# Ordered operand addresses at four places, a GpSimd fold for LayerNorm's sums and a later mean, in a decoder-layer kernel on Trainium2

## The chip, the core and the metric

The kernel runs on one core of one Trainium2 chip. The core has a tensor engine (PE) for matmuls, a vector engine (DVE), a scalar engine (ACT), GpSimd (POOL) and a sync engine (SP) that here only issues DMAs. Each works through its own instructions in order and waits on semaphores for the others. The metric is device time in microseconds (us), lower is better. A kernel is timed in several runs, and one execution is recorded by the hardware profiler; the start and end of every instruction in this document come from such a record.

## What is computed

One layer of a decoder over 288 tokens: 256 of one prompt and 8 x 4 of running samples. The width is 2048, everything is float32.

```python
h = rmsnorm(x, norm1_g)
proj = einsum("btd,de->bte", h, w_in) + b_in          # 2048 -> 3072
a, gate, z = proj[..., :1024], proj[..., 1024:2048], proj[..., 2048:]
u = a * sigmoid(gate)
u_ext = concat([hist_conv, u], axis=1)
c = silu(layernorm(depthwise_causal_conv(u_ext, conv_w, conv_b), ln_g, ln_b))   # 31 taps
z_ext = concat([hist_pool, z], axis=1)
d = multiscale_pool(z_ext, pos0)                      # windows 2, 4, 8, 16
p = einsum("btgc,gce->btge", d, pool_w) * pool_scale
x = x + einsum("btm,md->btd", concat([c, p], axis=-1), w_out)
h2 = rmsnorm(x, norm2_g)
f = square(relu(einsum("btd,df->btf", h2, w_ff1)))    # 2048 -> 8192
x = x + einsum("btf,fd->btd", f, w_ff2)               # 8192 -> 2048
```

A final RMSNorm follows. The last 30 rows of `u_ext` and the last 15 of `z_ext` are outputs too. LayerNorm runs over the 1024 convolution channels.

## The kernel before

**Layout.** Channels lie on the 128 partitions, tokens along the free dimension (`T` = 288), so each product is a 128x128 weight block against a 128x288 operand. All large products go through `gemm` (line 286), whose matmul is line 310.

**Three products for one.** float32 accuracy is made from the tensor engine's fast float32r format: a weight block is split into a high part (`whi`, a rounding copy on ACT, line 260) and a low part (`wlo`, the rest), and so are the operands. For every pair of reduction blocks and every output bank `gemm` issues six products: high by high, low weight by high operand, high weight by low operand, for two blocks each (`parts`, line 296). A call with two banks has 96 products for a reduction of 2048 (48 for 1024, 12 for a pooling group).

**Where the low part of a weight comes from.** `split_part` (line 254) knows three ways: "V", a subtraction on DVE (line 265); "G", two subtractions of 128x512 on GpSimd (line 268); "D", ACT writes the negative of the high part and a DMA that GpSimd issues adds the weight from memory (lines 262 and 263). `WAYS` (line 70) lists the ways by stage, in turn for the quarter-blocks (`wr`, 512 KB) of the stage: c3 has four of them, one gemm. Buffers: six raw blocks, five high and five low ones.

**The order of the operands.** `act2` (line 121) puts the high and low parts of two reduction blocks into one tile of four slots of 288 floats (1152 bytes): low even, high even, high odd, low odd. In the default order the products read slots 1, 2, 1, 2, 3, 0. `gemm` calls an operand class 0 if it lies in slot 1 or 3, else class 1; the default order thus alternates 0, 1, 0, 1. With `classes`, a string of digits, it reorders the first products of the call: for each digit it takes the next product of that class. Before uses this once, at chunk 0, g 2 of the first MLP product (line 603), with 24 digits.

**Stages.** The first gemm makes a and gate of convolution channels 0 and 1 (192 products, while x arrives). Then the sequence of line 45: `c2`, `c3`, `c4`, ... are 128 convolution channels each (`conv_products`, `conv_pair`), `p3` to `p0` the pooling groups (`pool_group`), `P3` to `P0` their small products (`pool_products`). The 31 taps of a convolution run on DVE, one instruction a tap (line 426), put behind all urgent work by `later()`. Channels 2j and 2j+1 share the tile `cs[j]`. `sum_c`, two halves of 288, gathers the sums of the even and the odd channel blocks as they finish, on GpSimd (line 435), up to channel block 5.

Then w_out comes in two halves. The pooling half (loop at line 543, eight g of 48 products, operands `dx`) runs first. LayerNorm's statistics stand between its products, by `BETWEEN` (line 541): `ln_mean` (line 517) at g 4 before reduction block 4, `ln_sums` at g 5 before block 6, `ln_rows` at g 6 before block 4. They are f32 matmuls with a matrix of 1/1024, which sum over partitions. `ln_sums` subtracts the mean, squares, adds up and starts the root; `ln_rows` spreads the root's 288 values over all partitions. `issue_after` keeps the products that follow on PE behind each. The normalized channels (`mixc`, lines 551 to 561) are the operands `mx` of the convolution half (loop at line 566, eight g of 48 products). The MLP runs in four chunks of 2048: eight g of 96 products from `ax` to `fx`, then eight g of 96 back. The row of the second RMSNorm (`rsqrt_rows`, line 605) stands between chunk 0, g 0 and g 1.

**Who sets the order.** The Tile framework orders the instructions of each engine by priority (program order, plus what `later` adds) over a simulated timeline, and sets the semaphores. Each engine then keeps that order on the chip.

Of the kernel before, what the change touches and what calls it, by code (L numbers as in the profile page):

```python
# [12 lines left out]
ALU = mybir.AluOpType  # L13
# [17 lines left out]
N8 = DC // P  # L31
# [35 lines left out]

WAYS = {"c2": "GVGV", "c3": "GDGD", "c4": "GDGD", "p3": "GDDG", "c5": "GDGD", "c": "GGGV", "p": "GVVG", "w": "GG", "ff": "VV"}  # L70


VEC = (("norm1_g", 16), ("b_in", 24), ("conv_b", 8), ("ln_g", 8), ("ln_b", 8), ("pool_scale", 8), ("norm2_g", 16), ("norm_f", 16))
# [10 lines left out]
def trunk_kernel(ctx: ExitStack, tc: tile.TileContext, io):  # L84
# [3 lines left out]
    nc = tc.nc  # L88
# [106 lines left out]
    ones = const.tile([P, P], F32, name="ones")  # L195
# [80 lines left out]
    def split(halves, stage="ff"):  # L276

        parts = []
        for raw, src in halves:
            turns[stage] = turns.get(stage, -1) + 1  # L280
            parts.append(spl())
            ways = WAYS.get(stage) or WAYS[stage[0]]
            split_part(raw, src, *parts[-1], ways[turns[stage] % len(ways)])
# [33 lines left out]
    def each(bk):  # L317
        return [bk[:, m, :] for m in range(2)]
# [28 lines left out]
    korder = [2 * g + m for g in GROUPS for m in range(2)]  # L347
# [43 lines left out]
    cs, pcs = [], []  # L391
    sum_c = tmpp.tile([P, 2, T], F32, name="sum_c", tag="ag2", bufs=2)
# [4 lines left out]
    def conv_products(i, **kw):  # L397
        history(i)
        banks = each(bank2())
        gemm(banks, hx, **kw)  # L400
        return banks

    def conv_pair(i, banks):
        up = u_all[:, i, 0:UO]
        us = samples(u_all[:, i, UO:UL], US)
        ta, gate = [b[:, :T] for b in banks]
        for b in (gate, ta):
            nc.vector.tensor_tensor(b, b, rb, op=ALU.mult)
        tg = tmpp.tile([P, 2, T], F32, name=nm("tg"), tag="ag", bufs=2)[:, 0, :]
        nc.scalar.activation(tg, gate, AF.Sigmoid, bias=v("b_in", 8 + i))  # L410
        if i == N8 - 1:
            load_table(AF.Sqrt, tg[:, 0:1])
        for out, a, b in ((up[:, CH:UO], ta[:, :SEQ], tg[:, :SEQ]), (us[:, :, CH:US], samples(ta[:, SEQ:T], NS), samples(tg[:, SEQ:T], NS))):
            nc.vector.scalar_tensor_tensor(out=out, in0=a, scalar=v("b_in", i), in1=b, op0=ALU.add, op1=ALU.mult)
        if i % 2 == 0:
            cs.append(actp.tile([P, 2, T], F32, name=nm("c"), tag="c", bufs=4))
        c = cs[i // 2][:, i % 2, :]
        with later():
            if i % 2 == 0:
                pcs.append(cvp.tile([P, 2, SEQ], F32, name=nm("pc"), tag="cv"))  # L420
            pc = pcs[i // 2][:, i % 2, :]
            cwv = vec[:, CWO + i * CW : CWO + (i + 1) * CW]
            nc.scalar.activation(pc, up[:, 0:SEQ], AF.Identity, bias=v("conv_b", i), scale=cwv[:, 0:1])  # L423
            for w in range(1, CW):
                dst = pc if w < CW - 1 else c[:, 0:SEQ]
                nc.vector.scalar_tensor_tensor(out=dst, in0=up[:, w : w + SEQ], scalar=cwv[:, w : w + 1], in1=pc, op0=ALU.mult, op1=ALU.add)  # L426
            prd = prdp.tile([P, NB, NS, CW + 1], F32, name=nm("prd"), tag="prd")
            nc.scalar.activation(prd[:, :, :, CW], ones[:, 0 : NB * NS].rearrange("p (b t) -> p b t", t=NS), AF.Identity, bias=v("conv_b", i), scale=0.0)
            for t in range(NS):
                nc.gpsimd.tensor_tensor(prd[:, :, t, 0:CW], us[:, :, t : t + CW], cwv[:, None, :].to_broadcast([P, NB, CW]), op=ALU.mult)  # L430
            cso = c[:, SEQ:T]
            nc.vector.tensor_reduce(samples(cso, NS), prd, axis=AX.X, op=ALU.add)
            if i % 2 and 1 < i < N8 - 1:
                for m in range(2):
                    nc.gpsimd.tensor_tensor(sum_c[:, m, :], (cs[0] if i == 3 else sum_c)[:, m, :], cs[i // 2][:, m, :], op=ALU.add)


    dd = {}
# [31 lines left out]
    mixp = {}  # L470
# [24 lines left out]
        return last  # L495

    with tc.issue_after(gemm(pair0 + pair1, hx, between={15: first_sums})):
        third = conv_products(2, between={2: first_rows})
    nc.gpsimd.memset(z_all[:, :, 0:PH], 0.0)
    conv_pair(0, pair0)  # L500
    conv_pair(1, pair1)
# [13 lines left out]
    norm = {}  # L515

    def ln_mean():
        nc.vector.tensor_tensor(sum_c, sum_c, cs[-1], op=ALU.add)  # L518
        nc.vector.tensor_tensor(sum_c[:, 0, :], sum_c[:, 0, :], sum_c[:, 1, :], op=ALU.add)  # L519
        norm["mean"] = ms("pmean")[:, 0, :T]  # L520
        return nc.tensor.matmul(norm["mean"], ones, sum_c[:, 0, :], start=True, stop=True)  # L521

    def ln_sums():
        ssc = None
# [13 lines left out]
        norm["rows"], last = spread(norm["sums"])  # L538
        return last

    BETWEEN = {4: {4: ln_mean}, 5: {6: ln_sums}, 6: {4: ln_rows}}
    behind = nullcontext()
    for g in range(8):
        bk = bank2()
        with behind:
            last = gemm(each(bk), [mixp[k] for k in korder], between=BETWEEN.get(g, {}))
        behind = tc.issue_after(last) if g > 3 else nullcontext()
        x2 = xT[:, 2 * g : 2 * g + 2, :]
        nc.vector.tensor_tensor(x2, x2, bk[:, :, :T], op=ALU.add)

    mixc = []
    for j, c in enumerate(cs):
        n = tmpp.tile([P, 2, T], F32, name=nm("n"), tag="ag", bufs=2)
        nc.vector.tensor_tensor(n, c, norm["rows"][:, None, :].to_broadcast([P, 2, T]), op=ALU.mult)
        for m in range(2):
            i = 2 * j + m
# [7 lines left out]
    x1 = []  # L564
    ss2 = row("ss2")
    for g in range(8):
        bk = bank2()
        gemm(each(bk), mixc)
        x2 = xT[:, 2 * g : 2 * g + 2, :]
        nc.vector.tensor_tensor(x2, x2, bk[:, :, :T], op=ALU.add)  # L570
        if g < 4:
            a2 = halves(act2("ax", tag="p", bufs=4))
        elif g < 6:
            if g == 4:
                ax45 = zp.tile([P, N8 * ZL], F32R, name="ax45", tag="z")
                ax45 = ax45[:, 32 : 32 + 8 * T].rearrange("p (g r t) -> p g r t", g=2, r=4)
            a2 = halves(rows(ax45[:, g - 4]))
        else:
            a2 = []
            for m in range(2):  # L580
                t2 = actp.tile([P, 2, T], F32R, name=nm("ax"), tag="c", bufs=4)
                a2.append((t2[:, 1 - m, :], t2[:, m, :]))
        for m, (ah, al) in enumerate(a2):
            k = 2 * g + m
            xk = xT[:, k, :]
            nc.scalar.activation(ah, xk, AF.Copy, scale=v("norm2_g", k))
            nc.vector.scalar_tensor_tensor(out=al, in0=xk, scalar=v("norm2_g", k), in1=f32(ah), op0=ALU.mult, op1=ALU.subtract)
            x1.append((ah, al))
            if k == 0:
                nc.scalar.activation(ss2, xk, AF.Square)  # L590
            else:
                q2 = tmp("q")
                nc.scalar.activation(q2, xk, AF.Square)
                nc.gpsimd.tensor_tensor(ss2, ss2, q2, op=ALU.add)
# [4 lines left out]
    for ch in range(DFF // FCH):  # L599
        fx = []  # L600
        for g in range(FCH // 256):
            bk = bank2()
            gemm(each(bk), x1, classes="01" + "110011001100" + "01" * 5 if ch == 0 and g == 2 else "")
            if ch == 0 and g == 0:
                nc.scalar.copy(r2, rsqrt_rows([ss2], 1.0 / D))
            t = tmpp.tile([P, 2, T], F32, name=nm("t"), tag="ag", bufs=2)
            nc.vector.scalar_tensor_tensor(out=t, in0=bk[:, :, :T], scalar=0.0, in1=both(r2), op0=ALU.max, op1=ALU.mult)  # L607
            f = tmpp.tile([P, 2, T], F32, name=nm("f"), tag="ag2", bufs=2)
            nc.scalar.activation(f, t, AF.Square)
            fh, fl = act2("fx")  # L610
            nc.scalar.copy(fh, f)
            nc.vector.tensor_tensor(fl, f, f32(fh), op=ALU.subtract)
            fx += halves((fh, fl))
        last = ch == DFF // FCH - 1
        for g in range(8):
            bk = bank2()
            banks = each(bk)
            if last and g == 7:
                banks[1] = bank2()[:, 1, :]
            gemm(banks, fx, m_outer=last and g == 7)  # L620
            for m in range(2):
                k = 2 * g + m
                xk = xT[:, k, :]
                if last:
                    nc.vector.tensor_tensor(xk, xk, banks[m][:, :T], op=ALU.add)
                    if k == 0:
                        nc.scalar.activation(ssf, xk, AF.Square)
                    else:
                        qf = tmp("q")
                        nc.scalar.activation(qf, xk, AF.Square)  # L630
                        if k < KT - 1:
                            nc.vector.tensor_tensor(ssf, ssf, qf, op=ALU.add)
                    nc.scalar.activation(xk, xk, AF.Copy, scale=v("norm_f", k))
                elif m:
                    x2 = xT[:, 2 * g : 2 * g + 2, :]
                    nc.vector.tensor_tensor(x2, x2, bk[:, :, :T], op=ALU.add)  # L636
# [65 lines left out]
```

## Time and profile before

| | us |
|---|---|
| three timed runs | 1096.64, 1096.86, 1117.09 |
| median of them | 1096.86 |
| the profiled execution, whole | 1097.78 |
| its span, first to last instruction | 1096.0 |
| DVE busy | 640.9 |
| ACT busy | 477.5 |
| GpSimd busy | 179.2 |
| mean granted clock of PE, as a share | 0.994 |

How to read the profile. A group row has line, engine, operation, output<-inputs by the program's names, shape, count, then total busy time, mean ns of one, and the idle time of the engine before them with what ended it. A chain row has start, length and what, one row for a run of equal instructions with their count. A window row has the window, its length, busy time of each engine with its count, the granted clock, the DMA engines' share and GB/s; a count takes in instructions that only reach into the window. "PEld" is the loading of weights, which overlaps with PE's products; matmuls overlap too, so the pace is time over count and not the length of one. A trailing q (POOLq) is an engine's sequencer.

### The profile page before, as it was taken

What the parts mean: (1) busy time and instruction counts of PE and PEld (TensorE: products, weight loads), DVE (VectorE), ACT (ScalarE), POOL (GpSimd) and SP (SyncE); (2) the same over time, 40 slices, a digit from 0 to 9 for tenths busy, and PEclk for the clock granted to TensorE, in tenths of its full rate; (3) what the DMA queues carried; (4) which work ended last, traced back from release to release, by engine and by line L of the source; (5) the groups of instructions that cost most, each with busy time, mean ns of one, the idle gap of its engine ahead of it and who ended that gap; (6) DMA issues with size and microseconds to landing.
All of it is one profiled execution on the core that took longest, in us unless ns stands there. A gap on an engine that the chain in (4) does not pass through costs nothing.

```text
span 1096.0 us, 19604 instructions
## 1 busy us (share of the span) xinstructions
PE 1077.8 (98%) x8204; PEld 1075.6 (98%) x8204; DVE 640.9 (58%) x814; ACT 477.5 (44%) x585; POOL 179.2 (16%) x209
## 2 busy tenths in 40 slices
PE   8999999899999999999999999999999999999996
PEld 8999999899999999999999999999999999999996
DVE  7889999778554544445554444445544445554553
ACT  8654445365444433334443333444433334444441
POOL 0878989602100000000000000000000000000000
PEclk9999999899999999999999999999999999999998
DMA  9996468455455555555555555555555555555522
GB/s 335 277 271 175 147 166 244 150 159 170 157 169 168 165 171 173 168 169 166 171 171 168 167 168 174 168 167 168 171 173 164 169 169 172 171 165 167 171 77 87
DMA packets 58264, 191.23 MB, mean 174 GB/s; under 512 B 6208, under 2 KB 11328, under 8 KB 58176
## 3 DMA queue, kind: packets, MB, share of 16 engines
q1 hardware_dynamic: 56752, 185.53, 54.0%
q0 software_dynamic: 1152, 4.19, 2.1%
q8 instruction: 64, 1.05, 0.4%
q10 hardware_dynamic: 272, 0.26, 0.1%
q14 instruction: 24, 0.20, 0.0%
HBM read 185.68 MB, written 4.28 MB: 173 GB/s over the span
## 4 chain that ended last, share of the span: by engine, by line
PE 95%; DMA 1%; DVE 1%; POOL 1%; issue 1%; ACT 0%; SPq 0%; DVEq 0%; POOLq 0%
PE ac L310 93%; DMA wlo<-in_w 1%; POOL wlo L268 1%; PE pp L310 0%; DVE xT L642 0%; DMA wr<-in_w 0%; POOL prd L430 0%; DVE sum_c L518 0%; PE pt L225 0%; ACT whi L260 0%; PE idle L228 0%; PE pt L245 0%; DVE sum_c L519 0%; PE pmean L521 0%; DVE wlo L265 0%
## 5 line engine op out<-in xcount | busy, mean ns | idle before, releaser
L260 ACT CAST whi<-wr 128x1024 fp32r<-128x1024 f32 (+1 forms) x341 | 355.1, 1041 | 566.2 <-PE ac L310 544.9
L265 DVE TENSOR_TENSOR wlo<-wr,whi 128x1024 fp32r<-128x1024 f32 (+1 forms) x295 | 363.3, 1232 | 352.5 <-ACT whi L260 352.1
L310 PE MATMUL ac<-ax,whi 128*128 128x288 f32 x2048 | 351.5, 292 | 0.0
L310 PE MATMUL ac<-fx,whi 128*128 128x288 f32 x2048 | 350.4, 292 | 0.0
L310 PEld LDWEIGHTS ac<-ax,whi 128*128 128x128 f32 x2048 | 296.0, 187 | 0.0
L310 PEld LDWEIGHTS ac<-fx,whi 128*128 128x128 f32 x2048 | 295.5, 187 | 0.0
L310 PE MATMUL ac<-ax,wlo 128*128 128x288 f32 x1024 | 217.1, 292 | 0.0
L310 PE MATMUL ac<-fx,wlo 128*128 128x288 f32 x1024 | 216.6, 292 | 0.0
L310 PEld LDWEIGHTS ac<-ax,wlo 128*128 128x128 f32 x1024 | 162.5, 187 | 0.0
L310 PEld LDWEIGHTS ac<-fx,wlo 128*128 128x128 f32 x1024 | 162.1, 187 | 0.0
L310 PE MATMUL ac<-hx,whi 128*128 128x288 f32 x768 | 136.5, 296 | 2.2 <-ACT hx L332 1.5
L310 PEld LDWEIGHTS ac<-hx,whi 128*128 128x128 f32 x768 | 114.0, 189 | 2.8 <-ACT hx L332 1.7
L268 POOL TENSOR_TENSOR wlo<-wr,whi 128x512 fp32r<-128x512 f32 x76 | 104.3, 1420 | 42.4 <-ACT whi L260 41.4
L426 DVE SCALAR_TENSOR_TENSOR pc<-u_all,vec,pc 128x256 f32<-128x256 f32 x232 | 99.7, 483 | 3.2 <-ACT pc L423 1.9
L310 PE MATMUL ac<-hx,wlo 128*128 128x288 f32 x384 | 85.5, 296 | 1.2 <-DMA wlo<-in_w 1.0
L310 PEld LDWEIGHTS ac<-hx,wlo 128*128 128x128 f32 x384 | 62.7, 189 | 1.7 <-DMA wlo<-in_w 1.3
L310 PE MATMUL ac<-dx,whi 128*128 128x288 f32 x256 | 47.6, 306 | 0.0
L310 PE MATMUL ac<-mx,whi 128*128 128x288 f32 x256 | 44.8, 296 | 0.0
L310 PEld LDWEIGHTS ac<-dx,whi 128*128 128x128 f32 x256 | 39.6, 197 | 0.3
L607 DVE SCALAR_TENSOR_TENSOR t<-ac,r 128x576 f32<-128x576 f32 x32 | 24.2, 758 | 26.4 <-PE ac L310 25.3
L310 PEld LDWEIGHTS ac<-mx,whi 128*128 128x128 f32 x256 | 37.7, 189 | 0.0
L636 DVE TENSOR_TENSOR xT<-xT,ac 128x576 f32<-128x576 f32 x24 | 18.1, 754 | 19.5 <-PE ac L310 19.5
(105 smaller groups left out, 507.7 us busy)
## 6 DMA issues: line engine op xcount, KB each, us to landing
wr<-in_w SPq DMA_DIRECT2D x335, 512.0 KB, 3.8
wlo<-in_w POOLq DMA_DIRECT2D x8, 512.0 KB, 7.6
xT<-in_xT SPq DMA_DIRECT2D x7, 288.0 KB, 8.2
wr<-in_w SPq DMA_DIRECT2D x5, 256.0 KB, 3.8
out_u_out<-u_all SPq DMA_DIRECT2D x1, 1208.0 KB, 10.5
out_yT<-xT SPq DMA_DIRECT2D x2, 576.0 KB, 2.9
u_all<-in_hist_c SPq DMA_DIRECT2D x8, 136.0 KB, 5.1
out_z_out<-z_all SPq DMA_DIRECT2D x1, 668.0 KB, 8.5
```

Of the source, the lines that this page charges most:

```text
L260: nc.scalar.copy(hi, raw)
L265: nc.vector.tensor_tensor(lo, raw, f32(hi), op=ALU.subtract)
L268: nc.gpsimd.tensor_tensor(lo[:, j : j + 2, :], raw[:, j : j + 2, :], f32(hi[:, j : j + 2, :]), op=ALU.subtract)
L310: last = nc.tensor.matmul(banks[m][:, :T], gets[k // 8](k % 8, m)[w], rhs[k][x], start=j == ends[m][0], stop=j == ends[m][1])
L426: nc.vector.scalar_tensor_tensor(out=dst, in0=up[:, w : w + SEQ], scalar=cwv[:, w : w + 1], in1=pc, op0=ALU.mult, op1=ALU.add)
L607: nc.vector.scalar_tensor_tensor(out=t, in0=bk[:, :, :T], scalar=0.0, in1=both(r2), op0=ALU.max, op1=ALU.mult)
L636: nc.vector.tensor_tensor(x2, x2, bk[:, :, :T], op=ALU.add)
```

## The change

`TURN` is a string of 48 digits with as many 0 as 1. It replaces the 24 digits in the first MLP product and is given to three other calls of `gemm`: the product of c2, behind 36 digits of the default order; the pooling half of w_out at g 2; the convolution half at g 2. No product is added or left out.

The fourth quarter-block of c3 gets its low part by GpSimd and not by the accumulating DMA.

When the even channel block 6 is done, GpSimd adds the odd half of `sum_c` and that block to the even half. `ln_mean` loses its two additions on DVE; it multiplies twice into the same bank, by the folded half and by channel block 7. Mean, sums and rows stand one g later, the rows before reduction block 2 in place of 4.

```diff
+TURN = "110100" * 4 + "01" * 6 + "1100" * 3
+
+
-WAYS = {"c2": "GVGV", "c3": "GDGD", "c4": "GDGD", ...
+WAYS = {"c2": "GVGV", "c3": "GDGG", "c4": "GDGD", ...
...
             if i % 2 and 1 < i < N8 - 1:
                 for m in range(2):
                     nc.gpsimd.tensor_tensor(sum_c[:, m, :], (cs[0] if i == 3 else sum_c)[:, m, :], cs[i // 2][:, m, :], op=ALU.add)
+            if i == N8 - 2:
+                for part in (sum_c[:, 1, :], c):
+                    nc.gpsimd.tensor_tensor(sum_c[:, 0, :], sum_c[:, 0, :], part, op=ALU.add)
...
-        third = conv_products(2, between={2: first_rows})
+        third = conv_products(2, between={2: first_rows}, classes="01" * 18 + TURN)
...
     def ln_mean():
-        nc.vector.tensor_tensor(sum_c, sum_c, cs[-1], op=ALU.add)
-        nc.vector.tensor_tensor(sum_c[:, 0, :], sum_c[:, 0, :], sum_c[:, 1, :], op=ALU.add)
         norm["mean"] = ms("pmean")[:, 0, :T]
-        return nc.tensor.matmul(norm["mean"], ones, sum_c[:, 0, :], start=True, stop=True)
+        nc.tensor.matmul(norm["mean"], ones, sum_c[:, 0, :], start=True, stop=False)
+        return nc.tensor.matmul(norm["mean"], ones, cs[-1][:, 1, :], start=False, stop=True)
...
-    BETWEEN = {4: {4: ln_mean}, 5: {6: ln_sums}, 6: {4: ln_rows}}
+    BETWEEN = {5: {4: ln_mean}, 6: {6: ln_sums}, 7: {2: ln_rows}}
...
-            last = gemm(each(bk), [mixp[k] for k in korder], between=BETWEEN.get(g, {}))
+            last = gemm(each(bk), [mixp[k] for k in korder], between=BETWEEN.get(g, {}), classes=TURN if g == 2 else "")
...
-        gemm(each(bk), mixc)
+        gemm(each(bk), mixc, classes=TURN if g == 2 else "")
...
-            gemm(each(bk), x1, classes="01" + "110011001100" + "01" * 5 if ch == 0 and g == 2 else "")
+            gemm(each(bk), x1, classes=TURN if ch == 0 and g == 2 else "")
```

More of the change, by code (lines that the diff above doesn't have):

```diff
@@ L66, in weight_blocks @@
                 yield "w_ff2", r, (c, c + P)
-WAYS = {"c2": "GVGV", "c3": "GDGD", "c4": "GDGD", "p3": "GDDG", "c5": "GDGD", "c": "GGGV", "p": "GVVG", "w": "GG", "ff": "VV"}
+TURN = "110100" * 4 + "01" * 6 + "1100" * 3
+WAYS = {"c2": "GVGV", "c3": "GDGG", "c4": "GDGD", "p3": "GDDG", "c5": "GDGD", "c": "GGGV", "p": "GVVG", "w": "GG", "ff": "VV"}
 VEC = (("norm1_g", 16), ("b_in", 24), ("conv_b", 8), ("ln_g", 8), ("ln_b", 8), ("pool_scale", 8), ("norm2_g", 16), ("norm_f", 16))
```

## The prediction

> **What bounds the kernel now.** I read the page's busy times and its chain of waits first, then the chain in order of time, then the tensor engine (PE) in windows and its waits.
>
> ```profile
> PE 1077.8 (98%) x8204; PEld 1075.6 (98%) x8204; DVE 640.9 (58%) x814; ACT 477.5 (44%) x585; POOL 179.2 (16%) x209
> ...
> PE 95%; DMA 1%; DVE 1%; POOL 1%; issue 1%; ACT 0%; SPq 0%; DVEq 0%; POOLq 0%
> ```
>
> PE is busy 98% of the span and makes 95% of the chain. So time can come from two things only: the few places where PE stops, and the pace of its products. The chain in order of time shows both (start, length, what; x is the number of instructions):
>
> ```profile
> 48.55 9.73 DMA wlo<-in_w
> ...
> 167.64 1.30 POOL wlo L268
> ...
> 198.53 2.63 DVE sum_c L518
> ...
> 201.19 1.41 DVE sum_c L519
> ...
> 202.64 1.33 PE pmean L521 x2
> 203.97 10.21 PE ac L310 x60
> ...
> 214.23 0.64 PE pt L225 x6
> 214.87 4.88 PE ac L310 x36
> 219.75 0.64 PE pt L245 x6
> 220.40 73.58 PE ac L310 x552
> ```
>
> The last row gives the pace of the products (line 310): 73.58 / 552 = 133.3 ns. The same products, of the same shape, in windows (length, PE busy with its count, granted clock, DMA share, GB/s):
>
> ```profile
> 62.00:162.00 100.00, 100.00 (x752) 1.00 0.66 182
> 196.00:210.00 14.00, 10.75 (x58) 0.76 0.49 161
> 223.50:293.80 70.30, 70.30 (x529) 1.00 0.54 165
> 320.00:1080.00 760.00, 760.00 (x5848) 1.00 0.52 163
> ```
>
> Rows one, three and four are gapless and at full clock, yet from 320 us on a product takes 760 / 5848 = 130.0 ns, against about 133 before. PE runs at two paces, 3.3 ns apart, and nothing in those rows but the stage tells them apart. The switch comes with the one place where before already orders the products by operand address (chunk 0, g 2 of the first MLP product); it then lasts to the end. Row two is the other loss: 14 us hold 56 products and the mean's two passes, at a mean clock of 0.76. At 133.3 ns the products need 7.5 us, so 6.5 us go to the mean, the wait before it and the lower clock. PE's waits from 40 to 240 us are these two:
>
> ```profile
> PE pmean L521 <- DVE sum_c L519: 3.2, 1, 3.2
> PE ac L310 <- DMA wlo<-in_w: 1.0, 1, 1.0
> ```
>
> **The change, part by part.**
>
> *LayerNorm's mean.* Removed: the two DVE adds of 2.63 and 1.41 us that stand between the last convolution tap and the mean. GpSimd gets two adds of 128x288 instead, earlier, and the mean becomes two matmuls. The mean also moves 48 products later, 6.4 us.
>
> ```profile
> L268 POOL TENSOR_TENSOR wlo<-wr,whi 128x512 fp32r<-128x512 f32 x76 | 104.3, 1420 | 42.4 <-ACT whi L260 41.4 <-issue 0.7
> ...
> L435 POOL TENSOR_TENSOR sum_c<-sum_c,c 128x288 f32<-128x288 f32 x2 | 1.6, 808 | 0.0
> ```
>
> PE reached the mean at 202.64 - 3.2 = 199.4. In the new place it arrives at 205.8, less what is won earlier (about 3 us, below), so near 202.7; its last operand, the end of convolution 7, was there at 198.5. The wait goes, with 4 us of slack, and with it the fall of the clock that follows it. The two folds cost 2 x 0.81 = 1.6 us on GpSimd; behind them queue the low parts for the pooling half, and their buffers hide it (price if not: 1.6 us of wait). The clock rule of the Trainium skill, "TensorE: Matmul & The Clock Gate", Part 1, says that the gate halves the clock after about one idle window of 3.4 us, in a free-running window; a 3.2 us wait followed by 0.76 agrees, and by it waits clearly shorter than that should leave the clock alone.
>
> The mean's matmul is f32 and runs as two passes, 1.33 us in all, at the lowered clock. Two matmuls are four passes: 2.7 us if they are no faster, 1.3 if the full clock halves them; I take 1.3, since the clock will not have fallen. Gain: 6.5 - 1.3 = 5.2 (3.8 to 5.2).
>
> *The later rows.* Mean to sums stays 60 products, sums to rows falls from 36 to 24, 3.2 us, and the root's steps on DVE must fit there:
>
> ```profile
> 214.91 0.16 DVE L231 TENSOR_SCALAR st<-pt 96x3 f32<-96x3 f32 x1 [0.82 <-PE pt L225]
> ...
> 216.71 0.16 DVE L238 SCALAR_TENSOR_TENSOR st<-st 96x3 f32<-96x3 f32 x1
> ```
>
> They took 2.0 us; 1.2 us stay free (no wait, or 0.5 where an add of x stands in between). Rows to the convolution half falls from 72 to 36, that is 36 x 0.133 = 4.8 us. What must fit there, on DVE:
>
> ```profile
> 220.43 1.42 DVE L554 TENSOR_TENSOR n<-c,pt 128x576 f32<-128x576 f32 x2 [1.36 <-PE pt L245]
> ...
> 224.32 0.75 DVE L560 TENSOR_TENSOR mx<-n,mx 128x576 fp32r<-128x576 f32 x1
> ...
> 232.28 0.75 DVE L560 TENSOR_TENSOR mx<-n,mx 128x576 fp32r<-128x576 f32 x1
> ```
>
> Counted from the end of the rows at 220.40, the first normalized pair is complete after 4.7 us and the fourth after 12.6. PE will ask for the first after 4.8 (just in time), and for the low part of the fourth after 4.8 + (36 + 8) x 0.133 = 10.7. So about 1.9 us of new wait, in pieces; nothing if ACT and DVE put these steps ahead of the next weights, 4 if they put more ahead of them. I take -2.0.
>
> *The low part of c3.* The wait of 1.0 us is for the fourth part of c3, whose low half came by an accumulating DMA issued at 48.55 and landed 9.73 us later. Two GpSimd subtractions of 1.42 us end before 52, when PE asks at 57. The wait goes: +1.0. But GpSimd issues c4's first such DMA behind them:
>
> ```profile
> 54.24 1.41 POOL L263 DMA_DIRECT2D wlo<-in_w  x1
> ```
> ```profile
> DMA to landing us min/median/max: 5.5/7.6/9.7
> ```
>
> It moves back by 2 x 1.42 - 1.4, about 1.4 us, and lands at 61.1 to 65.3, by the median at 63.2. PE was to ask for it at 58.3 + 48 x 0.133 = 64.7, now near 63.4. A new wait of 0 to 2; I take 0.3.
>
> *The sequences.* If a sequence sets the fast pace, it holds until PE is interrupted; every interruption before 300 us was followed by 133 again. Place 1 (c2, ends near 46 us) would run to where the last pooling products are mixed in (the row below): some 870 products x 3.3 ns = 2.9 us. Place 2 (pooling half, g 2) to the mean: 120 products, 0.4. Place 3 (convolution half, g 2) to the second RMSNorm's rows: 336 products, 1.1. Place 4 is where before already switches: 0. The sequences only reorder; they add no product.
>
> ```profile
> 163.88 0.42 PE L310 MATMUL pp<-dx,whi 128*128 128x288 f32 x2
> ```
>
> Of the 2.9 something is lost again at 168.95, where PE already waits for GpSimd's low parts (second fence). The engines from there on (PE, PEld, DVE, ACT, POOL):
>
> ```profile
> 143.60:169.00 25.40, 25.35 (x192) 25.12 (x190) 25.40 (x53) 11.77 (x18) 24.08 (x28) 1.00 0.71 180
> 162.30:185.50 23.20, 23.15 (x174) 22.90 (x173) 22.75 (x49) 13.04 (x17) 23.19 (x23) 1.00 0.89 239
> ```
>
> DVE and GpSimd are full, so within this stretch they can't follow a faster PE; their start can, since it hangs on buffers that PE releases. Over 25 us PE gains 2.5%: I take -0.5 (0 to -2).
>
> Sum: 5.2 - 2.0 + 1.0 - 0.3 + 2.9 - 0.5 + 0.4 + 1.1 = 7.8 us. The profiled run took 1097.78 (span 1096.0 and 1.8 around it), 0.9 above the median of 1096.86; against the median, 1089.
>
> **The rivals.**
>
> *The order of operands does not set the pace at places 1 to 3* (or the pace does not hold there). For: 130.0 was never seen before 300 us, and the switch was seen once, on MLP operands. Against: nothing else changes at the switch, and the clock is 1.00 on both sides. Then 5.2 - 2.0 + 0.7 = 3.9 is left: 1093. [...]
>
> *The late rows make one long wait.* The wait at the convolution half becomes 4 us in one piece and the clock falls as it did at 202: 0.24 x 14 = 3.4 us more. 7.8 - 2.0 - 3.4 leaves 2.4: 1094.5. For: DVE and ACT need 12.6 us where PE gives 10.7. Against: PE can start on the first pair.
>
> *The slower side: place 4 does not switch.* The new sequence of 48 replaces the 24 that worked. If PE stays at 133.3 ns after it, the some 6,000 products behind lose 20 us at one stroke: 1089 + 20 = 1109. It is decided at the first products after chunk 0, g 2. For: one of the three runs of before took 1117.09, 20.2 above the median, just this price, so even the old sequence may fail at times (no trace shows that run). Against: the new one ends in the same 110011001100 as the old.
>
> **How the numbers follow.** The forecast gets 0.55, the order without effect 0.19, the long wait 0.1, place 4 0.12, other things 0.04. Likeliest 1089, by its own bounds 1084 to 1093 (best: no new wait, 10.6 us, and 2 for differences between runs). With the next two cases the range is 1083 to 1098; place 4 stays out. Two per cent, about what a measurement of this kernel tells from no change, is 22 us. A gain of 22 is out of reach: all terms at their best give under 13. A loss of 22 needs place 4 to fail and the long wait on top. So faster 0.03, within 0.91, slower 0.06.
>
> **What would show it.** Right: no wait at pmean, and clock 1.00 from 196 to 210; gapless stretches at 130 ns from 46 to 160 us and from 245 to 285; no DMA wait in c3; a PE wait for mx near 220 of about 2 us in pieces. Wrong: 133 after a sequence; 133 after 320 us; a wait over 3 us at mx; a DMA wait in c4, after which the pace would be 133 up to place 2.

## The result, and the profile after

| | before | changed |
|---|---|---|
| median of 4 runs each, us | 1096.75 | 1087.83 |
| lowest, highest | 1094.93, 1117.09 | 1087.75, 1090.18 |
| profiled execution, its span | 1097.78, 1096.0 | 1087.89, 1086.1 |

The changed kernel takes 0.9929 of the time before, with a 95% interval of 0.9909 to 0.995: about 8 us less, within 2%. Over this whole study the kernel before was timed 53 times; four of these took 1115.5 to 1117.1 us (none of the four was profiled, and the mean granted clock on record for three of them is 0.996, no lower than in the others), and the ratios leave them out.

The page of the changed kernel, busy times and shares of the chain, beside which those of before stand in the prediction:

```profile
PE 1071.3 (99%) x8206; PEld 1069.0 (98%) x8206; DVE 632.8 (58%) x812; ACT 476.1 (44%) x584; POOL 181.5 (17%) x212
...
PE 96%; ACT 1%; DVE 1%; issue 1%; DMA 0%; POOL 0%; SPq 0%; DVEq 0%
```

PE is busy 6.5 us less, with two more instructions (the second matmul of the mean, in two passes); the rest of the gain is idle time. The windows of PE in the changed kernel (stretch, length, PE busy with its count, granted clock, DMA share, GB/s):

```profile
62.00:158.00 96.00, 96.00 (x740) 1.00 0.65 190
196.00:210.00 14.00, 14.00 (x105) 1.00 0.61 195
242.00:283.80 41.80, 41.80 (x324) 1.00 0.56 177
310.00:1070.00 760.00, 760.00 (x5848) 1.00 0.53 163
```

A count takes in about two products that only reach into the window, so row one is 96 / 738 = 130.1 ns and row three 129.8; before, 62 to 162 us held 752, less the same two, in 100 us: 133.3. From 196 to 210 us PE now has no idle time and a clock of 1.00, where it had 10.75 us busy and 0.76. The waits of PE between 40 and 300 us are down to one (total, times, longest):

```profile
PE ac L313 <- POOL wlo L271: 1.4, 1, 1.4
```

The chain of waits in order of time shows where it stands and what follows (start, length, what; line 313 is the product, before line 310):

```profile
111.23 24.96 PE ac L313 x192
136.19 1.56 PE pp L313 x12
137.75 21.55 PE ac L313 x166
...
164.71 1.27 POOL wlo L271
165.98 0.04 issue
166.02 3.72 PE ac L313 x26
...
172.41 27.06 PE ac L313 x206
199.47 0.48 PE pmean L525 x2
199.96 2.92 PE ac L313 x22
202.88 0.48 PE pmean L526 x2
203.37 4.87 PE ac L313 x37
208.23 1.61 issue
...
220.01 0.57 ACT mx L564
220.58 0.04 issue
220.62 63.43 PE ac L313 x480
```

24.96 / 192 = 130.0 ns. The low part that ends at 165.98 is the 1.4 us wait. The two matmuls of the mean stand apart: the scheduler put the first, which needs the fold alone, 22 products ahead of the second. From 208 to 220 the chain leaves PE for ACT and DVE, whose last step, an operand `mx`, ends 0.04 before the first product of the convolution half.

Products are never added or left out, so both traces can be cut at the start of the same product. That is the ledger of the gain, in blocks of 48 products (one g of w_out is a block, and the pooling half is blocks 25 to 32):

| stretch | before, us | changed, us | gain |
|---|---|---|---|
| up to c3 (blocks 0 to 5) | 47.26 | 47.11 | +0.15 |
| c3 (6, 7) | 14.09 | 12.48 | +1.61 |
| c4 and on (8 to 23) | 102.40 | 99.84 | +2.56 |
| 24, with the GpSimd wait | 6.67 | 8.02 | -1.35 |
| pooling half, g 0 to 3 | 25.61 | 25.36 | +0.25 |
| pooling half, g 4 to 7 | 33.82 | 27.82 | +6.00 |
| convolution half, g 0 | 6.40 | 6.82 | -0.42 |
| convolution half, g 1 and 2 | 12.76 | 12.77 | -0.01 |
| from there to the MLP's first g (36 to 42) | 45.25 | 44.13 | +1.12 |
| the rest | 801.74 | 801.77 | -0.03 |
| sum | | | +9.9 |

### The profile page after: what moved, and what is told of

Read it like the earlier page. It is cut to its first block, busy times and chain, and to the rows that moved or that the text cites. A ratio compares the mean times of both kernels' runs of the same rounds, so it can differ in the third digit from the quotient of the medians.

```text
span 1086.1 us, 19607 instructions
## 1 busy us (share of the span) xinstructions
PE 1071.3 (99%) x8206; PEld 1069.0 (98%) x8206; DVE 632.8 (58%) x812; ACT 476.1 (44%) x584; POOL 181.5 (17%) x212
## 4 chain that ended last, share of the span: by engine, by line
PE 96%; ACT 1%; DVE 1%; issue 1%; DMA 0%; POOL 0%; SPq 0%; DVEq 0%
PE ac L313 95%; PE pp L313 0%; DVE xT L647 0%; ACT whi L263 0%; DMA wr<-in_w 0%; DVE wlo L268 0%; POOL wlo L271 0%; PE idle L231 0%; ACT n L562 0%; PE pt L248 0%; PE pt L228 0%; ACT z_all L384 0%; ACT hx L335 0%; SPq L187 0%; DVE n L559 0%
## 5 line engine op out<-in xcount | busy, mean ns | idle before, releaser
L313 PE MATMUL ac<-dx,wlo 128*128 128x288 f32 x128 | 28.6, 297 | 1.4 <-POOL wlo L271 1.4
## 6 DMA issues: line engine op xcount, KB each, us to landing
out_u_out<-u_all SPq DMA_DIRECT2D x1, 1208.0 KB, 10.7
```

The source lines that it names most:

```text
L313: last = nc.tensor.matmul(banks[m][:, :T], gets[k // 8](k % 8, m)[w], rhs[k][x], start=j == ends[m][0], stop=j == ends[m][1])
```

## The experiments

Each kernel differs from the changed one by the lines shown. "Before" is the kernel before, timed beside it on the same chip.

| | median, lowest to highest, us | ratio to before, 95% interval |
|---|---|---|
| e1: no place 1 | 1090.67, 1089.78 to 1091.54 | 0.9939 [0.9924, 0.9954] |
| e2: no place 4 | 1109.27, 1107.78 to 1110.76 | 1.0108 [1.0093, 1.0124] |
| e3: DVE's adds, late | 1089.11, 1087.57 to 1090.63 | 0.9924 [0.9907, 0.9941] |
| e4: fold, old places | 1092.80, 1092.61 to 1093.70 | 0.9960 [0.9945, 0.9975] |
| e5: c3 by DMA | 1091.17, 1089.67 to 1092.60 | 0.9948 [0.9933, 0.9963] |
| e6: opening digits only | 1108.97, 1107.80 to 1110.26 | 1.0111 [1.0095, 1.0127] |
| e7: closing digits only | 1089.00, 1087.82 to 1089.74 | 0.9928 [0.9911, 0.9945] |
| e8: first low part of w_out by DVE | 1087.90, 1087.77 to 1091.61 | 0.9927 [0.9908, 0.9946] |
| e9: the changed kernel again | 1089.53, 1087.67 to 1090.78 | 0.9933 [0.9919, 0.9948] |
| e10: low parts of c4, p3 on DVE | 1092.34, 1091.08 to 1093.80 | 0.9960 [0.9947, 0.9974] |
| e11: e10 and more sequences | 1093.16, 1092.30 to 1095.00 | 0.9967 [0.9957, 0.9978] |
| e12: no DMA in c4 and p3 | 1096.12, 1095.66 to 1097.77 | 0.9993 [0.9984, 1.0002] |

### Does the order of the operands set the pace? (e1, e2, e6, e7)

**e1** takes the sequence out of c2, **e2** out of the MLP.

```diff
-        third = conv_products(2, between={2: first_rows}, classes="01" * 18 + TURN)
+        third = conv_products(2, between={2: first_rows})
```

> The changed kernel with the default order in c2 (place 1 undone), all else kept. Theory (the sequence sets the pace of PE's products): 133.3 ns a product from 46 us up to place 2 instead of 130.0, 2.9 us lost up to 160 us; the wait for GpSimd's low parts near 165 us shrinks from 1.4 to about 0.4, so 1.8 us slower than the changed kernel, about 1089.7. Rival (the order of operands does nothing): 130 ns in that stretch and 1088.

```diff
-            gemm(each(bk), x1, classes=TURN if ch == 0 and g == 2 else "")
+            gemm(each(bk), x1, classes="")
```

> The changed kernel with the default order in the first MLP product (place 4 undone). Theory: the second RMSNorm's rows near 290 us end the fast pace and nothing brings it back, so 133.3 ns a product to the end, some 6,000 products x 3.3 ns = 20 us slower, about 1108, the time of the one slow run of the kernel before. Rival (the pace comes with the MLP stage and not with the sequence): 130 ns and 1088.

Windows of PE in e1, and below them in e2:

```profile
62.00:158.00 96.00, 96.00 (x722) 1.00 0.65 189
```
```profile
62.00:158.00 96.00, 96.00 (x740) 1.00 0.65 190
...
310.00:1070.00 760.00, 760.00 (x5702) 1.00 0.51 164
```

Without its sequence each stretch falls back: 722 products in e1 where the changed kernel has 740, at the same clock and with no idle time; and 760 / 5702 = 133.3 ns in e2 where it has 130.0. The blocks 46 to 167 take 780.80 us in e2 and 761.28 in the changed kernel, 19.5 us, from one call of 48 reordered products. In e1 the stretch of block 24 falls from 8.02 to 6.66: PE arrives 2.9 us later, and the wait for GpSimd is gone. Net, place 1 is worth 1.6 us and not 2.9, since GpSimd's low parts take the other 1.3 back.

**e6** and **e7** keep one end of the 48 digits at place 4 and fill the rest with the default order.

```diff
-            gemm(each(bk), x1, classes=TURN if ch == 0 and g == 2 else "")
+            gemm(each(bk), x1, classes="110100" * 4 + "01" * 12 if ch == 0 and g == 2 else "")
```

> Place 4 gets the first 24 digits of the sequence and then the default order; the closing 110011001100 is left out there. If the closing digits make the switch (in the changed kernel 130 ns begins right behind them at each place): 133.3 ns to the end, about 1108. If the first digits already make it: 1088.

```diff
-            gemm(each(bk), x1, classes=TURN if ch == 0 and g == 2 else "")
+            gemm(each(bk), x1, classes="01" * 18 + "1100" * 3 if ch == 0 and g == 2 else "")
```

> Place 4 gets 36 digits of the default order and then 110011001100; the first 24 digits are left out there. If the closing digits are enough from any state: 1088 in every run. If they need the state that the first digits leave: 1108 in every run, or in some of the runs (the kernel before, which has only such closing digits, took 1117 in one of 11).

The opening digits alone do nothing that lasts (e6: 133.3 ns to the end), the closing ones alone do it all (e7: 761.28 us for blocks 46 to 167, like the changed kernel). The intervals from one product's start to the next, in ns, at the end of the 48 digits and after them, from the traces:

```
e7, last 12 of the 48     133 131 131 133 130 127 134 136 125 133 132 134
e7, the next 12           136 125 132 128 132 128 132 128 132 128 132 128
e6, last 12 of the 48     140 131 131 132 140 131 130 132 140 131 131 131
e6, the next 12           140 131 131 132 140 131 130 132 140 131 131 131
```

So the slow pace is a round of four (140, 131, 131, 131), one product in four about 9 ns late, and the fast one a round of two (132, 128; in the changed kernel's MLP 131, 129). Behind the closing digits the stream falls into the second round, and it stays there although the order is the default one again. At all four places of the changed kernel the intervals from the middle of the sequence on agree with each other to a few ns.

What these runs show is that the sequence sets the pace; that it does so by the operand's address is the idea behind it and is not shown. A digit moves a whole product, so the order of the weight halves changes with it, and in the closing twelve also the order of the output banks. By `gemm`'s code the twelve products of the default order, and every twelve of the opening digits, write six times to the first bank and then six times to the second; with 110011001100 the sixth already goes to the second bank and the seventh back to the first (the 24 digits of before mix the banks at one place too). The opening digits, which reorder operands and weights but not banks, do not make the switch, so the banks are a rival that no run here separates from the addresses.

In e6 and e7 something else was seen as well. Waits of PE from 40 to 300 us in e6, and windows of e7:

```profile
PE ac L313 <- DMA wlo<-in_w: 1.1, 1, 1.1
```
```profile
62.00:158.00 96.00, 96.00 (x723) 1.00 0.65 189
```

In e6 the first accumulating DMA of c4 landed late, at 64.2 us; PE waited 1.1 us at 63 and ran at 133 from there on. In e7 the fast pace ended near 75 us behind a product that began some 20 ns late (interval 152 for 131), in p3. It was the second product that reads a low part made by an accumulating DMA, which had landed at 75.14 us, 0.13 us before the first of these products; in the changed kernel the same DMA had landed 0.6 us ahead of need. Up to the MLP both are the program of the changed kernel.

### Is it the fold or the later place that removes the wait? (e3, e4)

**e3** undoes the fold (DVE's two additions and a single matmul are back) in the new places, **e4** keeps the fold in the old places.

```diff
-            if i == N8 - 2:
-                for part in (sum_c[:, 1, :], c):
-                    nc.gpsimd.tensor_tensor(sum_c[:, 0, :], sum_c[:, 0, :], part, op=ALU.add)
...
+        nc.vector.tensor_tensor(sum_c, sum_c, cs[-1], op=ALU.add)
+        nc.vector.tensor_tensor(sum_c[:, 0, :], sum_c[:, 0, :], sum_c[:, 1, :], op=ALU.add)
...
-        nc.tensor.matmul(norm["mean"], ones, sum_c[:, 0, :], start=True, stop=False)
-        return nc.tensor.matmul(norm["mean"], ones, cs[-1][:, 1, :], start=False, stop=True)
+        return nc.tensor.matmul(norm["mean"], ones, sum_c[:, 0, :], start=True, stop=True)
```

> The changed kernel with the two DVE additions and the single mean matmul back, GpSimd's fold left out, mean, sums and rows in their new places. If the later place is what removes the wait: the last tap ends at 195.2 us, the additions at about 199.5, PE arrives at 202.9: no wait, clock 1.00, within 1 us of 1088. If the fold is needed: a wait of about 3 us at the mean and the lower clock, about 1094.

```diff
-    BETWEEN = {5: {4: ln_mean}, 6: {6: ln_sums}, 7: {2: ln_rows}}
+    BETWEEN = {4: {4: ln_mean}, 5: {6: ln_sums}, 6: {4: ln_rows}}
```

> The changed kernel with mean, sums and rows back in their old places, GpSimd's fold and the two mean matmuls kept. If the fold alone is enough: PE reaches the mean at about 196 us, the last tap ends at about 195.2 us, so a wait under 1 us and clock 1.00; the 0.7 us of waits for the first normalized channels go too: 1087 to 1088.5. If the later place is needed: a wait of 2 to 3 us at the mean, a lower clock behind it, 1091 to 1094.

e3, the DVE's timeline (start, length, line, operation) and the window of PE around it:

```profile
197.19 5.37 DVE L521 TENSOR_TENSOR sum_c<-sum_c,c 128x576 f32<-128x576 f32 x1
...
202.59 1.43 DVE L522 TENSOR_TENSOR sum_c<-sum_c 128x288 f32<-128x288 f32 x1
```
```profile
194.00:214.00 20.00, 20.00 (x154) 1.00 0.60 195
```

The two additions take 6.8 us, 2.8 more than before, and still end at 204.0, just ahead of the mean at 204.21: no idle time, clock 1.00. Blocks 30 to 33 are 0.45 us shorter than in the changed kernel, 0.42 of it in the block that has one matmul of the mean less. So in the new place the fold buys nothing that can be measured; the later place alone removes the wait.

e4 went another way than I expected. Its window of PE and its waits from 40 to 300 us:

```profile
194.00:214.00 20.00, 17.79 (x122) 0.91 0.55 181
```
```profile
PE pt L228 <- DVE q L538: 2.2, 1, 2.2
PE ac L313 <- POOL wlo L271: 1.4, 1, 1.4
```

The wait at the mean is gone here too (PE reaches it at 197.8), but one of 2.2 us stands at the next step, the sums, and the clock halves behind it from 209.7 to 213.2. The DVE had the squares, which ACT makes, to add up while GpSimd was at work; its timeline in e4, and the same steps in the changed kernel, a g later:

```profile
198.81 2.75 DVE L531 TENSOR_TENSOR c<-c,pmean 128x576 f32<-128x576 f32 x4 [1.89 <-PE pmean L526]
201.47 2.38 DVE L537 TENSOR_TENSOR q<-q,q 128x576 f32<-128x576 f32 x1
...
207.43 1.40 DVE L538 TENSOR_TENSOR q<-q 128x288 f32<-128x288 f32 x1
```
```profile
209.75 0.74 DVE L537 TENSOR_TENSOR q<-q,q 128x576 f32<-128x576 f32 x1
210.52 0.46 DVE L538 TENSOR_TENSOR q<-q 128x288 f32<-128x288 f32 x1
```

The first addition takes 2.38 us in e4, where those of the same size take 0.74 in the changed kernel once GpSimd is done; the last one takes 1.40 and 0.46. The two between them in e4 took 1.18 and 1.66. GpSimd ran low parts without a gap from 196.95 to 209.95 in e4, but was done at 206.7 in the changed kernel. The Trainium skill, "GPSIMD Engine Reference", Key points, says that GpSimd shares its SBUF interfaces with VectorE and that they contend where a DVE instruction has two inputs from SBUF; these additions have two, and the rows agree, with factors of 1.6 to 3.2 that the section does not give. The four subtractions in the first row, of the same size but with one input from PSUM (`pmean`), took 0.75 us each beside the same GpSimd work. Fold and place together make blocks 29 to 33 last 34.6 us, the fold alone 38.0, neither 40.2.

### The low part of c3 and the wait for GpSimd (e5, e8)

```diff
-WAYS = {"c2": "GVGV", "c3": "GDGG", "c4": "GDGD", "p3": "GDDG", "c5": "GDGD", "c": "GGGV", "p": "GVVG", "w": "GG", "ff": "VV"}
+WAYS = {"c2": "GVGV", "c3": "GDGD", "c4": "GDGD", "p3": "GDDG", "c5": "GDGD", "c": "GGGV", "p": "GVVG", "w": "GG", "ff": "VV"}
```

> The changed kernel with the fourth low part of c3 by the accumulating DMA again. If a wait ends the fast pace: the wait of 1.0 to 1.3 us near 57 us is back, 133 ns a product behind it up to place 2 (2.6 us), and the wait for GpSimd near 165 us shrinks by about 1: 2.7 us slower than the changed kernel, about 1090.7. If the pace survives a wait: 1.3 slower, about 1089. If GpSimd's queue gives c4's DMA its earlier start back and something else hides it: 1088.

Waits of PE in e5 from 40 to 300 us, and its window behind c3:

```profile
PE ac L313 <- DMA wlo<-in_w: 0.3, 1, 0.3
```
```profile
62.00:158.00 96.00, 96.00 (x722) 1.00 0.65 187
```

The DMA cost only 0.3 us of wait in this execution, but it ended the fast pace of place 1 at 58.6 us: c3 takes 13.10 us for 12.48, and all that follows up to block 24 runs at 133. Of place 1 almost nothing is left in this execution, so this edit is what place 1 stands on.

```diff
-WAYS = {"c2": "GVGV", "c3": "GDGG", "c4": "GDGD", "p3": "GDDG", "c5": "GDGD", "c": "GGGV", "p": "GVVG", "w": "GG", "ff": "VV"}
+WAYS = {"c2": "GVGV", "c3": "GDGG", "c4": "GDGD", "p3": "GDDG", "c5": "GDGD", "c": "GGGV", "p": "GVVG", "w0": "VG", "w": "GG", "ff": "VV"}
```

> The changed kernel with the first half of the first w_out block split by DVE in place of GpSimd. If the 1.4 us wait near 165 us is GpSimd being behind: it goes, about 1086.5, and the last tap ends about 1 us later, still ahead of the mean. If DVE, full in that stretch, delivers no earlier: the same wait, now for DVE, and 1088 or slightly more.

The 1.4 us wait becomes one of 0.5 and two smaller, block 24 falls from 8.02 to 7.09, and blocks 25 to 27 rise from 19.12 to 19.71: 0.3 us in all. In the changed kernel the engines were this full there (PE, PEld, DVE, ACT, POOL):

```profile
143.60:169.00 25.40, 23.99 (x184) 23.76 (x183) 25.40 (x54) 11.55 (x17) 24.08 (x27) 1.00 0.72 187
```

DVE has not a moment free, so the work only changes hands.

### The changed kernel once more (e9)

> The changed kernel again, unaltered, as the control of the next two and for its spread. In the profiles so far the accumulating DMAs of c4 and p3 land 0.6 to 1.0 us before PE asks for them, and in two of ten profiles one came late and the pace was 133 ns from there to place 2. If that is where the spread comes from, the runs lie on levels: 1087.8, about 1.7 more where the clock is halved for 3.4 us at the start, and 2 to 3 more where a DMA is late; 1087.7 to 1091.5.

Its trace repeats the changed kernel's, block by block within 0.03 us from block 1 on, except at the start. The first 21 us in e9, and below them in the first profile of the changed kernel:

```profile
0.00:21.00 21.00, 17.57 (x102) 0.92 0.92 328
```
```profile
0.00:21.00 21.00, 18.09 (x118) 1.00 0.91 327
```

In e9 the clock was half from 12.4 to 15.8 us and block 0 took 11.46 us for 9.23. That accounts for the 2.2 us between the two profiled executions, and e1 to e5 have it too. Differences under some 2 us between medians are therefore read from the ledger and not from the times.

### What could be had beyond it (e10, e11, e12)

e10 gives DVE the low parts that stood closest to being late. e11 does so too, moves the sequence of the convolution half to g 1, and puts one at g 1 of every MLP chunk. e12 has no accumulating DMA in c4 and p3 at all. The diff of e11 leaves out the line of `WAYS`, which is that of e10.

```diff
-WAYS = {"c2": "GVGV", "c3": "GDGG", "c4": "GDGD", "p3": "GDDG", "c5": "GDGD", "c": "GGGV", "p": "GVVG", "w": "GG", "ff": "VV"}
+WAYS = {"c2": "GVGV", "c3": "GDGG", "c4": "GVGD", "p3": "GVDG", "c5": "GDGD", "c": "GGGV", "p": "GVVG", "w": "GG", "ff": "VV"}
```

> The changed kernel with the second low part of c4 and of p3 by DVE in place of the accumulating DMA. If the thin margin of these DMAs causes the late ones: no DMA wait and 130 ns from 47 to 159 us in the profile, the level 2 to 3 us above is gone, median 1087.5 to 1088.5 with less spread. If DVE, 95% busy there, falls behind: a wait of PE for DVE in c4 or p3, or the last tap after 203 us, and 1089 or more.

```diff
-        gemm(each(bk), mixc, classes=TURN if g == 2 else "")
+        gemm(each(bk), mixc, classes=TURN if g == 1 else "")
...
-            gemm(each(bk), x1, classes=TURN if ch == 0 and g == 2 else "")
+            gemm(each(bk), x1, classes="01" * 24 + TURN if g == 1 else "")
```

> As the previous kernel, and the sequence at g 1 in place of g 2 of the convolution half, and in the second half of g 1 in all four chunks of the first MLP product (before: chunk 0, g 2 alone). If the sequence makes the fast pace from any state and keeps it: the fast pace starts 48 products earlier at two places, 0.2 to 0.3 us less, and three more sequences in a stream that is fast already cost under 0.1 us each: 1087 to 1088. If a sequence in the fast stream ends the pace: 133 ns behind chunk 1, about 1100 or more.

```diff
-WAYS = {"c2": "GVGV", "c3": "GDGG", "c4": "GDGD", "p3": "GDDG", "c5": "GDGD", "c": "GGGV", "p": "GVVG", "w": "GG", "ff": "VV"}
+WAYS = {"c2": "GVGV", "c3": "GDGG", "c4": "GVGV", "p3": "GVVG", "c5": "GDGD", "c": "GGGV", "p": "GVVG", "w": "GG", "ff": "VV"}
```

> The changed kernel with all four accumulating DMAs of c4 and p3 replaced by DVE's subtraction. In the run with two of them replaced, a product of the convolution's sample part stood ahead of the DMA in GpSimd's queue and waited 6.4 us for DVE. Without any DMA there: if the pace needs only that PE is never kept waiting, 130 ns from 47 to 159 us, none of the runs with a late DMA, 1087.5 to 1089. If DVE's order puts these subtractions behind too many taps: PE waits for DVE in c4 or p3, the pace is 133 from there, 1090 or more.

All three are slower than the changed kernel. Waits of PE in e10 from 40 to 300 us, and the timeline of GpSimd ahead of the longer one:

```profile
PE ac L313 <- DMA wlo<-in_w: 2.5, 1, 2.5
PE ac L313 <- POOL wlo L271: 0.3, 1, 0.3
```
```profile
69.62 3.66 POOL L433 TENSOR_TENSOR prd<-u_all,vec 128x248 f32<-128x248 f32 x4 [6.38 <-DVE u_all L417]
73.23 0.86 POOL L266 DMA_DIRECT2D wlo<-in_w  x1
```

and its chain:

```profile
73.23 7.73 DMA wlo<-in_w
```

The remaining DMA of p3 is issued at 73.23 and lands at 80.96, 7.73 us later. It stood on GpSimd's queue behind four products of the convolution, and these waited 6.38 us for `u_all`, which DVE now made later. The clock was half from 81.0 to 84.4 us, and the pace 133 afterwards. In e12 the same queue holds back the first DMA of c5, with a wait of 3.1 us. Its windows:

```profile
48.00:84.00 36.00, 36.00 (x279) 1.00 0.46 152
84.00:96.20 12.20, 9.13 (x58) 0.86 0.96 226
96.20:120.00 23.80, 23.80 (x185) 1.00 0.47 152
129.00:160.00 31.00, 31.00 (x235) 1.00 0.53 170
```

Up to 84 us the pace is kept through c4 and p3, as meant. Then come the wait and 3.4 us at half clock; and behind them the pace is 23.8 / 183 = 130 ns again (about two of the 185 only reach into it), with no sequence there. It is lost near 121.6 us, where PE waits 0.8 us for an operand `dx`.

In e11 the sequences of the later chunks cost under 0.1 us each and change nothing. At g 1 of the convolution half the sequence failed:

```profile
242.00:283.00 41.00, 41.00 (x309) 1.00 0.57 179
```

41 / 308 = 133 ns, and blocks 36 to 42 take 45.25 us, as before the change. Products of g 0 that wait for the last `mx` are mixed into that call, and an interval of 202 ns stands right behind the closing digits; that these broke the sequence is argued from the trace, not shown.

## Why the prediction was right, step by step

1089 was forecast by a sum of 7.8 us and 0.9 for the profiled execution of before being above its median; 1087.83 came, and the ledger has 9.9 for the profiled executions. Three terms were mis-sized: LayerNorm and the low part of c3 gave 2.8 us more than forecast, GpSimd took 0.85 more. That the forecast came within 1.2 us is in part luck: these errors partly cancel, and the 0.9 covers a part of what remains (the changed kernel's profiled execution, 1087.89, lies at its median).

| term | predicted | measured |
|---|---|---|
| LayerNorm: mean, rows and `mx` | 5.2 - 2.0 = 3.2 | 5.4 |
| c3 and c4 | 1.0 - 0.3 = 0.7 | 1.3 |
| place 1 | 2.9 | 3.0 |
| GpSimd near 165 us | -0.5 | -1.35 |
| place 2 | 0.4 | 0.3 |
| place 3 | 1.1 | 1.1 |
| place 4 | 0 | 0 |
| elsewhere | | 0.1 |

Worked from the ledger: of c3's 1.61 us, 0.32 are place 1 (96 products x 3.3 ns) and 1.29 the low part; place 1 is 0.09 at the end of c2, that 0.32, and 2.56. Place 2 is 0.16 in each of two blocks. LayerNorm is 6.00 - 0.16 - 0.42.

**The mean.** Right: no wait, clock 1.00 from 196 to 210. The cause was the later place, by e3; the fold, to which the prediction gave the removed additions, was not needed for it. It counts only in the old place, where e4 shows the wait going on to the sums. The two matmuls cost 0.95 us, not 1.3: the block that holds both takes 7.35 us, where 48 products alone take 6.40.

**The later rows.** The wait for `mx` was taken as 2.0 and was about 0.7: 0.25 in the last block of the pooling half, which has the rows now (7.30 us, where the block with the rows took 7.05 before), and 0.42 in the first of the convolution half (6.82 for 6.40). The step that failed counted ACT's and DVE's steps from the end of the rows at the pace of before, 12.6 us for four pairs, against 10.7; the pieces are where it said and are a third as long.

**c3 and c4.** The wait in c3 went. The wait in c4, put at 0 to 2 with 0.3 taken, was absent in the profiled execution, but the DMA landed 1.0 us ahead of need (62.0 for 63.0) where it had 1.5 before, and in e6 it came late, with the loss of the pace that the prediction named as what would prove it wrong.

**GpSimd near 165 us.** The size was off: PE arrives 2.9 us earlier and waits 1.4 in one piece; the prediction let GpSimd follow PE too far. Counted from the start of c3, the low part that PE waits for ended at 118.9 us and in e1 at 120.4: GpSimd came 1.5 us earlier for PE's 2.9. e1 shows the size from the other side, e8 that DVE has no room for it.

**The sequences.** The step "if a sequence sets the fast pace" is shown for places 1 and 4 by e1, e2, e6 and e7; places 2 and 3 rest on the ledger, place 3 also on e11, where the sequence failed and the pace stayed at 133. That the operand's address is what acts is not shown (the banks, above). "Every interruption is followed by 133 again" holds in the profile of before, but not always: e12 came out of a wait and a half clock at 130 ns.

**The rivals.** The order without effect fell by e1 and e2. The long wait at `mx` did not come. Place 4 not switching did not come, and its price of 20 us was right: e2 and e6, which do not switch, lie 19.5 us behind in those blocks. One argument against it was misread: the 24 digits of before do not end in 110011001100 but go on with ten digits of the alternating order behind it. The price is also about what separates the four long times of the kernel before from its others; since none of them was profiled, whether its 24 digits failed there stays open. None of the 49 timings of kernels with the 48 digits at that place was so long, which is too few to settle it.

**The clock.** The prediction took from the Trainium skill, "TensorE: Matmul & The Clock Gate", Part 1, that an idle window of about 3.4 us halves the clock, and inferred that clearly shorter waits leave it alone. Here waits of 1.0 (before), 1.1 (e6), 1.2 (e12) and 1.4 us (the changed kernel) left it at 1.00, but 2.2 (e4, e11), 2.5 (e10) and 3.1 us (e12) each brought 3.4 us at half clock, and the 3.2 us of before 6.8. The measurement decides: in this kernel 2.2 us of waiting was enough.

Not settled: what in the reordered products (operand addresses, output banks or weights) chooses a round of two or of four, and why a product 20 ns late ended the fast one in e7, while the twelve pooling products in the middle of the stretch (the chain of the changed kernel has 130 ns on both sides of those at 136.19) did not end it.

## What to carry to other kernels

Where a gapless stream at full clock shows two paces, look at the intervals of single products, not at the waits: a few reordered products may be worth more (20 us here) than every wait that the page lists. Such a pace hangs on what comes before it, so a wait of 0.3 us can cost ten times its length, and a DMA that lands 0.6 us early in one execution is not safe: in another it had 0.13 us left, and the pace was lost. And a step that is made earlier for one engine is worth only what the next one can follow: read which engines are full in the stretch, and what else stands on the queue that issues the DMAs.

## What the runs showed of the hardware that was not expected

- Two stable paces of the same product at one clock: 133.3 and 130.0 ns, as rounds of four (140, 131, 131, 131) and of two (132, 128), chosen by twelve reordered products ahead of them.
- Half a clock behind every wait of 2.2 us and more between 40 and 300 us: for 3.4 us behind 2.2 to 3.1 us, for 6.8 behind 3.2; none behind waits of 1.4 us and less.
- An f32 addition of 128x576 on DVE with both inputs in SBUF took 0.74 us beside an idle GpSimd and 1.2 to 5.4 us (e4, e3) while GpSimd subtracted; a subtraction of that size with one input in PSUM took 0.75 beside a busy GpSimd (e4).
- A half clock of 3.4 us between 12 and 16 us in some executions and not in others of the same kernel, worth about 2 us of its time.
